# A hybrid decoder block: the last block of the down stages read straight from its accumulator, and the recurrence's gate matmuls on two row halves

## The chip, the core and the metric

The kernel runs on one core of one Trainium2 chip. Its engines work side by side and wait for each other by semaphores: PE (TensorE, matrix products; PEld is its weight load), DVE (VectorE, elementwise work), ACT (ScalarE, activation functions and copies), POOL (GpSimd) and SP (SyncE, which here issues DMAs). Products go to PSUM, an accumulator memory of eight banks; everything else lies in SBUF. The metric is the device time of one execution in microseconds (us); smaller is better.

## What is computed

A block of one layer on 512 tokens of width 1024, all in float32. It is a sum of three steps onto the residual stream, each with a norm before and a norm after:

```python
f = swiglu(rms_norm(h, ffn1_pre_g), ffn1_w_gu, ffn1_w_down)      # width 2816
h = h + 0.5 * rms_norm(f, ffn1_post_g)
m = hybrid_mixer(rms_norm(h, mix_pre_g), ...)
h = h + rms_norm(m, mix_post_g)
f = swiglu(rms_norm(h, ffn2_pre_g), ffn2_w_gu, ffn2_w_down)
h = h + 0.5 * rms_norm(f, ffn2_post_g)
```

The mixer runs a recurrence and a sliding-window attention on the same input and merges them by gates. The recurrence's part that matters here:

```python
xc = causal_depthwise_conv(x_br, conv_w, conv_b)
r = sigmoid(block_diag_linear(xc, w_a, b_a))      # 16 heads of 64 channels, a 64 x 64 matrix each
i = sigmoid(block_diag_linear(xc, w_x, b_x))
log_a = -8 * r * softplus(-lam); a = exp(log_a)
h_t = a_t * h_(t-1) + sqrt(max(1 - a_t**2, 0)) * (i_t * xc_t)
```

## The kernel before, in words

**Products.** Every float32 operand is split into a high part and a low part (a cast on ACT, a subtraction on DVE), and a product is three matmuls: high x high, high x low, low x high (`mm3`, L147 to L150). Weights come from HBM by DMAs on SP (`wload`, L98, three ahead of the splits), are split by `wsplit` (cast L109, subtraction L110), and `wget` (L115) hands them out in one fixed order with two splits ahead.

**The down stages.** The second product of each feed-forward block is done by `down` (L529) as a 2 x 2 block product with seven products instead of eight. Its accumulators are X, Y and Q, each of two banks (two tiles of 128 tokens); products go in the order 1, 2, 3, 6, 5, 7, 4 (L622 to L660). `snap` (L601) copies an accumulator to SBUF, `plus` (L606) adds one to such a copy. Product 7 gives the last of the blocks for tiles 0 and 1, product 4 that for tiles 2 and 3. After product 7, ACT copies X (L645), DVE subtracts the copy "p" and then Q (L647, L648). The whole stretch stands in a block with an order written out by hand (L621): each engine's instructions keep the order in which they are written.

**Closing a stage.** `boundary` (L469) closes each of the three steps; b1 follows the first down stage, b2 the mixer's output product, b3 the second down stage. `half(t, i, z)` (L482) takes half the columns of tile t: a sum of squares on ACT (L489) and the product with the norm's gain on DVE (L490). `epilogue(t)` (L498) computes the inverse norm (a tensor_scalar on DVE, L495, and a power on POOL, L193), adds to the residual (L507), squares again (L512), computes the second inverse norm and multiplies by it and the next gain (L520). Then it hands back a number, FEATURE_LAG, of ticks to wait; a tick is one call of `tick` (L137), made after each piece of weights. Then `to_features` (L202) transposes the tile on PE (L207), casts it to the high part on ACT (L211) and subtracts for the low part on DVE (L212); for b2 it also copies the raw values on ACT (L214). `run` (L123) traces all steps of an epilogue up to that number at once, so they stand in the queues ahead of all that is written later.

In b1 tile 0 waits 6 ticks and tile 1 waits 10. Product 4 takes six pieces for tile 2, then six for tile 3. So tile 0's transposes come right after tile 2's product, and tile 1's after four pieces of tile 3's.

**The mixer.** The first four chunks of the recurrence's input are made by `first_four` (L225), in two halves of the tokens: the first half needs tiles 0 and 1 of the normalised input u2, high and low parts. `lru_chunk` (L817) does a chunk of 128 channels (two heads): convolution (L820 to L823), split (L825, L826), gate matmuls (L836, L837), tanh of each gate (L839, L841), and the factors of the recurrence (L842 to L846). The gate weights are one 128 x 128 matrix per chunk and gate, with the two heads' 64 x 64 matrices on its diagonal and zeros elsewhere. They come by two DMAs of 512 KB (L813), are split at the first chunk (L828 to L831), and each gate of a chunk is one `mm3` into a bank of its own: r in one bank, i in the other, 128 rows each. The last chunk of each group of four starts the scans (L849 to L856).

**Order.** Outside the hand-ordered blocks a planner lists the instructions by its own estimate of times; it may also put instructions from outside into the gaps of a hand-ordered block. PSUM banks and SBUF buffers are given out as they come free.

Of the kernel before, what the change touches and what calls it, by code (L numbers as in the profile page):

```python
# [10 lines left out]
AF = mybir.ActivationFunctionType  # L11
ALU = mybir.AluOpType
# [4 lines left out]
P = 128  # L17
# [2 lines left out]
TAILS = 7  # L20
WARM = 10
JSTD = {"f1": 6, "f2": 4}
FEATURE_LAG = {"b1": (6, 10, 7, 3), "b2": (3, 3, 3, 4)}
ATT_GATES = (2, 3, 4, 5, 6, 7)
T = 512
NT = T // P
D = 1024
# [15 lines left out]
def hybrid_block_kernel(ctx, tc, x, xt, g1, w_first, gains, gu1, gs1, dn1, w_x, w_gate, w_q, w_k, w_v, w_gl, w_ga, w_pl, w_pa,  # L43
# [156 lines left out]
        return u[part][k // 4][:, k % 4, tok]  # L200

    def to_features(un, t, u, name, raw=None):  # L202
        for half in range(2):
            b = bank(f"{name}tp{t}{half}")
            for i in range(4):
                k = 4 * half + i
                PE.transpose(out=b[:, i * P:(i + 1) * P], in_=un[:, k * P:(k + 1) * P], identity=ident)  # L207
# [3 lines left out]
            A.copy(uh, bv)  # L211
            V.tensor_tensor(out=ul, in0=bv, in1=uh.bitcast(F32), op=ALU.subtract)  # L212
            if raw is not None:
                A.copy(raw[half][:, :, ts_], bv)  # L214

    def feat_chunk(b, w, u, tok):
        wh, wl = w
# [251 lines left out]
    def boundary(src, dst, g_post, g_pre, u, scale, name, raw=None, then=None):  # L469
# [7 lines left out]
                rhs.append(rh)  # L477

        cols = (slice(0, 512), slice(512, 1024))
        sq, parts = {}, {}  # L480

        def half(t, i, z, sign=1.0, o=None):  # L482
            if t not in sq:
                sq[t], parts[t] = sm(f"{name}ps{t}", 2), [None, None]
            if o is None:
                while len(rhs) <= t:
                    residual()
                o = rhs[t][:, 1, cols[i]]
            A.activation(t4(f"{name}sq{t}{i}")[:, :512], z, AF.Square, scale=1.0 / 32.0, accum_out=sq[t][:, i:i + 1])  # L489
            V.scalar_tensor_tensor(out=o, in0=z, scalar=sign * scale, in1=g_post[:, cols[i]], op0=ALU.mult, op1=ALU.mult)  # L490
            parts[t][i] = o

        def inverse(ms, z):
            me = sm(f"{name}{z}e")
            V.tensor_scalar(out=me, in0=ms[:, 0:1], scalar1=ms[:, 1:2], scalar2=EPS, op0=ALU.add, op1=ALU.add)  # L495
            return rstd(me, f"{name}{z}r")

        def epilogue(t):  # L498
            while len(rhs) < min(t + 2, NT):
                residual()  # L500
            res, h = rhs[t][:, 0, :], rhs[t][:, 1, :]
            r = inverse(sq[t], f"p{t}")
            yield
            if g_pre is not None:
                ms, un = sm(f"{name}ms{t}", 2), t4(f"{name}un{t}")
            for i in range(2):
                V.scalar_tensor_tensor(out=h[:, cols[i]], in0=parts[t][i], scalar=r, in1=res[:, cols[i]],  # L507
                                       op0=ALU.mult, op1=ALU.add)
                if g_pre is None:
                    (SP if i == 0 else A).dma_start(dst[t][:, cols[i]], h[:, cols[i]])  # L510
                else:
                    A.activation(un[:, cols[i]], h[:, cols[i]], AF.Square, scale=1.0 / 32.0, accum_out=ms[:, i:i + 1])  # L512
            if g_pre is None:
                return
            A.dma_start(dst[t], h)
            yield
            r = inverse(ms, f"n{t}")
            yield
            for i in range(2):
                V.scalar_tensor_tensor(out=un[:, cols[i]], in0=h[:, cols[i]], scalar=r, in1=g_pre[:, cols[i]],  # L520
                                       op0=ALU.mult, op1=ALU.mult)
# [7 lines left out]
    def down(ps, name):  # L529
# [91 lines left out]
        with tc.manual_schedule():  # L621
            for i in (1, 2, 3, 6, 5, 7):  # L622
                for c in range(2 * (i == 1), KS if i < 7 else KS - 3, 2):
                    if i == 7 and c < 4:
                        half(2 + c // 2, 0, sn["a"][c // 2], 1.0, sn["a"][c // 2])
                    if i == 7 and c >= 4:
                        half(c // 2 - 2, 0, sn["c"][c // 2 - 2])
                    piece(i, c)
                if i == 1:
                    snap("a", X)  # L630
                elif i == 2:
                    plus("a", Y)
                elif i == 3:
                    snap("p", Q)
                elif i == 6:
                    snap("c", X)
                elif i == 5:
                    plus("c", Q)
            w = [wget(), wget()]
            prep[7][4]()  # L640
            for t in range(2):
                for c in range(KS - 3, KS):
                    unit(7, c, w[c // (KS - 1)], (t,))
            wsplit(wpos[0] + 4)
            snap("z", X)  # L645
            for t in range(2):
                V.tensor_tensor(out=sn["z"][t], in0=sn["z"][t], in1=sn["p"][t], op=ALU.subtract)  # L647
                V.scalar_tensor_tensor(out=sn["z"][t], in0=Q[t], scalar=-1.0, in1=sn["z"][t], op0=ALU.mult,  # L648
                                       op1=ALU.subtract)
                half(t, 1, sn["z"][t])  # L650
            wsplit(wpos[0] + (KS + 1) // 2)
            run(epilogue(t) for t in range(2))
            ws = []
            for t in range(2):
# [155 lines left out]

    bdt = []
    bdraw = []
    for i in range(2):  # L813
        bdraw.append(t4(f"bdraw{i}"))
        SP.dma_start(bdraw[i], bd[i])

    def lru_chunk(c, b, a4, m4, bx4, last):  # L817
        i = c % 4
# [13 lines left out]
                bdt.append(t)  # L832
        yield LRU_LAG[c // 4]
        cb = slice(c * P, (c + 1) * P)
        br, bi = bank(f"r{c}"), bank(f"i{c}")
        mm3(br, bdt[0][:, 0, cb], bdt[0][:, 1, cb], xh, xl, True, True)  # L836
        mm3(bi, bdt[1][:, 0, cb], bdt[1][:, 1, cb], xh, xl, True, True)  # L837
        tr = t2(f"tr{c}")
        A.activation(tr, br, AF.Tanh, scale=0.5, bias=hb[:, 0, c:c + 1])  # L839
# [263 lines left out]
    dn_run[0].send(boundary(hs2, ov, g_post, None, None, 0.5, "b3"))  # L1103


_VECS = ["conv_b", "lru_b_a", "lru_b_x", "lru_lambda"]


def _layout(inputs):
# [51 lines left out]
    vec = [f["conv_w"][i] for i in range(4)] + [f[n] for n in _VECS]  # L1161
    a["vecs"] = c(np.stack(vec).reshape(8, KD, P).transpose(2, 0, 1))
    bd = np.zeros((2, 2, HD, KD, 2, HD), np.float32)
    wb = np.stack([f["lru_w_a"], f["lru_w_x"]]).reshape(2, KD, 2, HD, HD)
    for r in range(2):
        bd[:, r, :, :, r, :] = wb[:, :, r].transpose(0, 2, 1, 3)
    a["bd"] = bd.reshape(2, P, D)
# [32 lines left out]
```

## Time and profile before

| | us |
|---|---|
| three runs | 1124.97, 1128.05, 1125.46; median 1125.46 |
| the profiled execution | 1124.96 |
| its span, first to last instruction | 1123.2 |
| mean granted TensorE clock in it | 0.997 of full speed |
| PE busy | 1103.9 |
| DVE busy | 896.4 |
| ACT busy | 593.9 |

All times in the rows are counted from the span's start. A row of a timeline has: start, duration, engine, line, operation, output<-inputs, shape, how many rows were merged, and in brackets how long the engine was idle before it and what ended that. A row of the waits has: who waited, for whom, us in total, times, the longest. A row of the windows has: the stretch and its length, then busy time and number of instructions for PE, PEld, DVE, ACT and POOL, then the granted clock, the DMA share and GB/s. A row of a tile has durations in ns (least, median, most), the first and the last start. Matmuls are pipelined: the duration of one is longer than the distance from one start to the next.

### The profile page before, as it was taken

To read this page: it belongs to the slowest core of one execution; us is meant where nothing else is said; L and a number is where in the kernel's file an instruction comes from. 1 tells how busy PE (TensorE), PEld (TensorE's weight loads), DVE (VectorE), ACT (ScalarE), POOL (GpSimd) and SP (SyncE) were. 2 spreads that over 40 slices of the span, in tenths; PEclk is the share of its full clock that TensorE was granted. 3 is DMA by queue.
4 is the path that set the end of the run, shared out by engine and by line. 5 is a ranking of instruction groups with operands and counts; after the bars stand their busy time and mean duration, and the time that the engine had idled before them with its cause. 6 is when DMAs were issued, how large, how long until landed. Compare 5 with 4: busy or idle time off the path is not lost.

```text
span 1123.2 us, 16795 instructions
## 1 busy us (share of the span) xinstructions
PE 1103.9 (98%) x6558; PEld 983.4 (88%) x6558; DVE 896.4 (80%) x1277; ACT 593.9 (53%) x995; POOL 79.5 (7%) x82
## 2 busy tenths in 40 slices
PE   9999999999989999999999999999999999999997
PEld 7889999988868888887888888887999999998885
DVE  6998898888998698999777561556858889888896
ACT  7445555475755658466455341335434455456571
POOL 1000000000001001114022000000000000000000
PEclk9999999999999999999999999999999999999999
DMA  9239999665676272711822340533348999455573
GB/s 359 83 121 261 312 284 302 180 225 150 208 270 213 89 205 76 206 57 57 249 87 86 123 157 31 189 111 113 113 125 261 271 312 282 138 163 189 161 264 113
DMA packets 53279, 202.07 MB, mean 180 GB/s; under 512 B 6352, under 2 KB 6480, under 8 KB 48464
## 3 DMA queue, kind: packets, MB, share of 16 engines
q1 hardware_dynamic: 45424, 163.77, 43.4%
q0 software_dynamic: 3456, 23.07, 10.5%
q10 hardware_dynamic: 4320, 14.16, 3.6%
q8 instruction: 51, 0.84, 0.3%
q14 instruction: 28, 0.23, 0.1%
HBM read 189.44 MB, written 57.67 MB: 220 GB/s over the span
## 4 chain that ended last, share of the span: by engine, by line
PE 84%; DVE 10%; issue 2%; ACT 2%; POOL 1%; DMA 0%; DVEq 0%; POOLq 0%; ACTq 0%
PE f2X L150 4%; PE f2X L149 4%; PE f2X L148 4%; PE f1X L150 4%; PE f1X L149 4%; PE f1X L148 4%; DVE w L110 3%; PE f2Q L150 2%; PE f2Q L149 2%; PE f2Q L148 2%; PE f1Q L150 2%; PE f1Q L149 2%; PE f1Q L148 2%; PE f1f L761 2%; PE x L149 1%
## 5 line engine op out<-in xcount | busy, mean ns | idle before, releaser
L110 DVE TENSOR_TENSOR w<-wraw,w 128x1024 fp32r<-128x1024 f32 x168 | 197.1, 1194 | 38.7 <-ACT w L109 36.9
L109 ACT CAST w<-wraw 128x1024 fp32r<-128x1024 f32 x168 | 163.5, 1011 | 27.7 <-PE glp L150 7.1
L150 PE MATMUL f1X<-u1m,f1W 128*128 128x256 f32 x256 | 72.5, 283 | 0.1
L149 PE MATMUL f1X<-u1m,f1W 128*128 128x256 f32 x256 | 72.4, 283 | 0.0
L148 PE MATMUL f1X<-u1m,f1W 128*128 128x256 f32 x256 | 72.4, 283 | 0.0
L150 PEld LDWEIGHTS f1X<-u1m,f1W 128*128 128x128 f32 x256 | 49.1, 192 | 0.3 <-DVE f1W L316 0.3
L148 PEld LDWEIGHTS f1X<-u1m,f1W 128*128 128x128 f32 x256 | 49.1, 192 | 0.1
L149 PEld LDWEIGHTS f1X<-u1m,f1W 128*128 128x128 f32 x256 | 49.1, 192 | 0.1
L150 PE MATMUL f2X<-u3m,f2W 128*128 128x256 f32 x144 | 40.9, 284 | 0.1
L150 PE MATMUL f2X<-u3h,f2W 128*128 128x256 f32 x144 | 40.8, 283 | 0.0
L148 PE MATMUL f2Q<-u3m,f2W 128*128 128x256 f32 x144 | 40.8, 283 | 0.0
L149 PE MATMUL f2Q<-u3m,f2W 128*128 128x256 f32 x144 | 40.8, 283 | 0.0
L150 PE MATMUL f2Q<-u3m,f2W 128*128 128x256 f32 x144 | 40.8, 283 | 0.0
L149 PE MATMUL f2X<-u3l,f2W 128*128 128x256 f32 x144 | 40.8, 283 | 0.0
L148 PE MATMUL f2X<-u3m,f2W 128*128 128x256 f32 x144 | 40.8, 283 | 0.0
L149 PE MATMUL f2X<-u3m,f2W 128*128 128x256 f32 x144 | 40.7, 283 | 0.0
L148 PE MATMUL f2X<-u3h,f2W 128*128 128x256 f32 x144 | 40.7, 283 | 0.0
L148 PE MATMUL f1Q<-u1m,f1W 128*128 128x256 f32 x128 | 36.2, 283 | 0.0
L149 PE MATMUL f1Q<-u1m,f1W 128*128 128x256 f32 x128 | 36.2, 283 | 0.0
L150 PE MATMUL f1Q<-u1m,f1W 128*128 128x256 f32 x128 | 36.2, 283 | 0.0
L149 PE MATMUL f1X<-w,f1y 128*128 128x512 f32 x88 | 35.0, 397 | 0.6 <-DVE w L110 0.6
L148 PE MATMUL f1X<-w,f1y 128*128 128x512 f32 x88 | 35.1, 398 | 0.0
(847 smaller groups left out, 3753.9 us busy)
## 6 DMA issues: line engine op xcount, KB each, us to landing
wraw<-wsum SPq DMA_DIRECT2D x40, 512.0 KB, 4.0
wsum<-in_dn_dram SPq DMA_DIRECT2D x16, 1024.0 KB, 9.0
wraw<-in_dn_dram SPq DMA_DIRECT2D x30, 512.0 KB, 5.0
f2L<-in_gs_dram SPq DMA_DIRECT2D x18, 512.0 KB, 5.0
f2R<-in_gs_dram SPq DMA_DIRECT2D x18, 512.0 KB, 5.1
wraw<-in_gu_dram SPq DMA_DIRECT2D x16, 512.0 KB, 5.8
f1L<-in_gs_dram SPq DMA_DIRECT2D x16, 512.0 KB, 5.5
f1R<-in_gs_dram SPq DMA_DIRECT2D x16, 512.0 KB, 5.7
```

The source lines that it names most:

```text
L109: A.copy(w[:, 0, :], raws[n])
L110: V.tensor_tensor(out=w[:, 1, :], in0=raws[n], in1=w[:, 0, :].bitcast(F32), op=ALU.subtract)
L148: PE.matmul(o, lhsT=ah, rhs=bh, start=start, stop=False, skip_group_check=reopen)
L149: PE.matmul(o, lhsT=ah, rhs=bl, start=False, stop=False, skip_group_check=reopen)
L150: PE.matmul(o, lhsT=al, rhs=bh, start=False, stop=stop, skip_group_check=reopen)
L761: PE.matmul(bs[i], lhsT=lw[:, i * P:(i + 1) * P], rhs=rx, start=k == 0 and n == 0, stop=k == KD - 1 and n == 2)
```

## The change

- **Down stages.** Q - p is computed right after product 5, into p. After product 7 one operation per tile takes -X - p straight from the accumulator; the copy of X and one subtraction per tile are gone. All six weight splits of product 4 are asked for ahead of the last matmuls of product 7 instead of four ahead and two behind the halves. The first halves of tiles 2 and 3 are done at product 6, those of tiles 0 and 1 at the first two pieces of product 7.
- **`half` and `epilogue`.** For the second half of the columns the gain is kept back and done in the epilogue, behind the tensor_scalar and the issue of the power. This holds at all three closings.
- **`to_features`.** Where raw copies are wanted, they come after both halves' casts and subtractions.
- **FEATURE_LAG.** b1: tile 0 waits 7 ticks and tile 1 waits 9; b2: tile 3 waits 3.
- **The gates.** The weights are one 128 x 1024 array: the rows are a head's 64 input channels for the even heads, then for the odd ones; for each chunk the columns are 64 outputs of gate r and 64 of gate i. A chunk's matmuls use 64 rows each, alternately of the first and the second head, and each head has its own bank with r in the lower half of the partitions and i in the upper half. The two tanh over 128 partitions become four over 64, two of which write to another half than they read. One DMA, one cast and one subtraction load the weights instead of two each. The biases are laid out to match.

```diff
-FEATURE_LAG = {"b1": (6, 10, 7, 3), "b2": (3, 3, 3, 4)}
+FEATURE_LAG = {"b1": (7, 9, 7, 3), "b2": (3, 3, 3, 3)}
...
     def to_features(un, t, u, name, raw=None):
+        keep = []
...
             if raw is not None:
-                A.copy(raw[half][:, :, ts_], bv)
+                keep.append((raw[half][:, :, ts_], bv))
+        for z, bv in keep:
+            A.copy(z, bv)
...
-        sq, parts = {}, {}
+        sq, parts, late = {}, {}, {}
...
             A.activation(t4(f"{name}sq{t}{i}")[:, :512], z, AF.Square, scale=1.0 / 32.0, accum_out=sq[t][:, i:i + 1])
-            V.scalar_tensor_tensor(out=o, in0=z, scalar=sign * scale, in1=g_post[:, cols[i]], op0=ALU.mult, op1=ALU.mult)
             parts[t][i] = o
+
+            def gain():
+                V.scalar_tensor_tensor(out=o, in0=z, scalar=sign * scale, in1=g_post[:, cols[i]], op0=ALU.mult,
+                                       op1=ALU.mult)
+
+            if i == 0:
+                gain()
+            else:
+                late[t] = gain
...
             r = inverse(sq[t], f"p{t}")
+            late[t]()
             yield
...
                 for c in range(2 * (i == 1), KS if i < 7 else KS - 3, 2):
+                    if i == 6 and c < 4:
+                        half(2 + c // 2, 0, sn["a"][c // 2], 1.0, sn["a"][c // 2])
                     if i == 7 and c < 4:
-                        half(2 + c // 2, 0, sn["a"][c // 2], 1.0, sn["a"][c // 2])
-                    if i == 7 and c >= 4:
-                        half(c // 2 - 2, 0, sn["c"][c // 2 - 2])
+                        half(c // 2, 0, sn["c"][c // 2])
                     piece(i, c)
...
                 elif i == 5:
                     plus("c", Q)
+                    for t in range(2):
+                        V.tensor_tensor(out=sn["p"][t], in0=Q[t], in1=sn["p"][t], op=ALU.subtract)
             w = [wget(), wget()]
             prep[7][4]()
+            wsplit(wpos[0] + (KS + 1) // 2)
             for t in range(2):
                 for c in range(KS - 3, KS):
                     unit(7, c, w[c // (KS - 1)], (t,))
-            wsplit(wpos[0] + 4)
-            snap("z", X)
             for t in range(2):
-                V.tensor_tensor(out=sn["z"][t], in0=sn["z"][t], in1=sn["p"][t], op=ALU.subtract)
-                V.scalar_tensor_tensor(out=sn["z"][t], in0=Q[t], scalar=-1.0, in1=sn["z"][t], op0=ALU.mult,
-                                       op1=ALU.subtract)
-                half(t, 1, sn["z"][t])
-            wsplit(wpos[0] + (KS + 1) // 2)
+                z = sn["p"][t]
+                V.scalar_tensor_tensor(out=z, in0=X[t], scalar=-1.0, in1=z, op0=ALU.mult, op1=ALU.subtract)
+                half(t, 1, z)
             run(epilogue(t) for t in range(2))
...
-    for i in range(2):
-        bdraw.append(t4(f"bdraw{i}"))
-        SP.dma_start(bdraw[i], bd[i])
+    bdraw.append(t4("bdraw"))
+    SP.dma_start(bdraw[0], bd)
...
-        br, bi = bank(f"r{c}"), bank(f"i{c}")
-        mm3(br, bdt[0][:, 0, cb], bdt[0][:, 1, cb], xh, xl, True, True)
-        mm3(bi, bdt[1][:, 0, cb], bdt[1][:, 1, cb], xh, xl, True, True)
+        heads = (slice(0, HD), slice(HD, P))
+        bs = [bank(f"ri{c}{r}") for r in range(2)]
+        for n, (w, x) in enumerate(((0, xh), (0, xl), (1, xh))):
+            for r, own in enumerate(heads):
+                PE.matmul(bs[r], lhsT=bdt[0][own, w, cb], rhs=x[own, :], start=n == 0, stop=n == 2)
         tr = t2(f"tr{c}")
-        A.activation(tr, br, AF.Tanh, scale=0.5, bias=hb[:, 0, c:c + 1])
         ti = bx4[:, i, :]
-        A.activation(ti, bi, AF.Tanh, scale=0.5, bias=hb[:, 1, c:c + 1])
+        for z, o in enumerate((tr, ti)):
+            for r, own in enumerate(heads):
+                A.activation(o[own, :], bs[r][heads[z], :], AF.Tanh, scale=0.5, bias=hb[heads[z], r, c:c + 1])
```

The rest of the diff lays out the gate weights and the biases in that order on the host.

More of the change, by code (lines that the diff above doesn't have):

```diff
@@ L1103, in hybrid_block_kernel @@
     dn_run[0].send(boundary(hs2, ov, g_post, None, None, 0.5, "b3"))
-_VECS = ["conv_b", "lru_b_a", "lru_b_x", "lru_lambda"]
 def _layout(inputs):
@@ L1160, in _layout @@
     a["dn2"] = down_blocks(f["ffn2_w_down"])
-    vec = [f["conv_w"][i] for i in range(4)] + [f[n] for n in _VECS]
+    gates = np.stack([f["lru_b_a"], f["lru_b_x"]]).reshape(2, KD, 2, HD).transpose(2, 1, 0, 3).reshape(2, D)
+    vec = [f["conv_w"][i] for i in range(4)] + [f["conv_b"], gates[0], gates[1], f["lru_lambda"]]
     a["vecs"] = c(np.stack(vec).reshape(8, KD, P).transpose(2, 0, 1))
-    bd = np.zeros((2, 2, HD, KD, 2, HD), np.float32)
     wb = np.stack([f["lru_w_a"], f["lru_w_x"]]).reshape(2, KD, 2, HD, HD)
-    for r in range(2):
-        bd[:, r, :, :, r, :] = wb[:, :, r].transpose(0, 2, 1, 3)
-    a["bd"] = bd.reshape(2, P, D)
+    a["bd"] = c(wb.transpose(2, 3, 1, 0, 4).reshape(P, D))
     a["sinks"] = f["attn_sinks"]
```

## The prediction

> **What bounds the kernel now.** I read the page first, then the waits of PE, then the timeline of each stage where PE waits, because only there can a change of order pay.
>
> ```profile
> span 1123.2 us, 16795 instructions
> ...
> PE 1103.9 (98%) x6558; PEld 983.4 (88%) x6558; DVE 896.4 (80%) x1277; ACT 593.9 (53%) x995; POOL 79.5 (7%) x82
> ```
>
> TensorE is busy in 98% of the span. So there are two ways to gain: take matmul time away, or take away one of the few waits of PE. The waits of PE, longest first (us in total, times, longest):
>
> ```profile
> PE b1ntp L207 <- DVE b1un L520: 4.8, 2, 3.8
> PE f2f L148 <- ACT u3h L211: 1.5, 1, 1.5
> ...
> PE q L148 <- DVE at01pl L978: 1.3, 1, 1.3
> PE at02t L975 <- POOL at02s L969: 1.2, 1, 1.2
> PE f1X L149 <- DVE w L110: 0.6, 1, 0.6
> PE f2X L149 <- DVE w L110: 0.6, 1, 0.6
> PE f2f L149 <- DVE u3l L212: 0.4, 1, 0.4
> ```
>
> The first row, the join of the first feed-forward block to the mixer (b1), is the largest. The two rows of w L110 are the start of the last product of the two down stages. The rows of f2f are the join b2. The rows of q and at02t stand in the mixer, where DVE has a backlog. PE at b1:
>
> ```profile
> 332.24 0.39 PE L150 MATMUL f1X<-w,f1y 128*128 128x512 f32 x1
> 336.39 1.32 PE L207 MATMUL b1ntp<-ident,b1un 128*128 128x128 f32 x8 [3.76 <-DVE b1un L520]
> ...
> 338.10 0.63 PE L150 MATMUL f1X<-w,f1y 128*128 128x512 f32 x1
> ...
> 340.66 0.63 PE L150 MATMUL f1X<-w,f1y 128*128 128x512 f32 x1
> ...
> 347.33 0.39 PE L150 MATMUL f1X<-w,f1y 128*128 128x512 f32 x1
> ...
> 350.82 0.29 PE L149 MATMUL x<-u2l,w 128*128 128x256 f32 x1
> ```
>
> PE stands at tile 0's transposes for 3.8 us. After that seven matmuls, from 338.10 to 340.66, start 0.43 us apart instead of 0.227 (1.36 us for six, shown below): the granted clock was halved after the pause, and that costs 7 x 0.2 = 1.4 us more. Then the mixer's first product does not run freely until 350.82.
>
> **The down stages.** What DVE and ACT do before those transposes:
>
> ```profile
> 321.70 2.35 DVE L110 TENSOR_TENSOR w<-wraw,w 128x1024 fp32r<-128x1024 f32 x2
> ...
> 324.69 0.69 DVE L648 SCALAR_TENSOR_TENSOR f1z<-f1Q,f1z 128x512 f32<-128x512 f32 x1
> ...
> 329.23 1.83 DVE L110 TENSOR_TENSOR w<-wraw,w 128x1024 fp32r<-128x1024 f32 x2 [1.07 <-ACT w L109]
> 330.98 0.20 DVE L495 TENSOR_SCALAR b1p0e<-b1ps 128x1 f32<-128x1 f32 x1
> ...
> 331.93 1.42 DVE L507 SCALAR_TENSOR_TENSOR b1rh<-b1rh,b1p0r 128x512 f32<-128x512 f32 x2 [0.62 <-POOL b1p0r L193]
> ...
> 335.60 1.40 DVE L520 SCALAR_TENSOR_TENSOR b1un<-b1rh,b1n0r,g_b 128x512 f32<-128x512 f32 x2
> ...
> 338.24 2.35 DVE L110 TENSOR_TENSOR w<-wraw,w 128x1024 fp32r<-128x1024 f32 x2
> ...
> 342.43 2.35 DVE L110 TENSOR_TENSOR w<-wraw,w 128x1024 fp32r<-128x1024 f32 x2
> 345.22 0.75 DVE L507 SCALAR_TENSOR_TENSOR b1rh<-f1a,b1p2r,b1rh 128x512 f32<-128x512 f32 x1 [0.44 <-POOL b1p2r L193]
> ...
> 348.56 1.41 DVE L520 SCALAR_TENSOR_TENSOR b1un<-b1rh,b1n2r,g_b 128x512 f32<-128x512 f32 x2 [0.66 <-POOL b1n2r L193]
> 349.89 1.28 DVE L212 TENSOR_TENSOR u2l<-b1ntp,u2h 128x512 fp32r<-128x512 f32 x2
> ```
> ```profile
> 324.22 0.59 ACT L604 COPY f1z<-f1X 128x512 f32<-128x512 f32 x1 [1.45 <-PE f1X L150]
> 325.48 0.63 ACT L489 ACTIVATE b1sq<-f1z 128x512 f32<-128x512 f32 x1 [0.67 <-DVE f1z L648]
> 326.01 0.19 ACT L489 ACTIVATION_READ_ACCUMULATOR b1sq<-f1z 128x1 f32 x1
> ```
>
> ACT copies the second part of X at 324.22, as soon as PE has finished it; DVE is at its splits until 321.70 + 2.35 = 324.05, so the two arrive together. The change removes, behind the last matmul of product 7, two copies on ACT and two subtractions on DVE (the latter move ahead of product 7). The two gains of the second halves move behind the tensor_scalar, beside POOL's power. The two splits of 329.23 come forward. The working for the changed order:
>
> DVE ends its four splits at 324.05 + 1.83 = 325.9; X is complete by then, so it does L648 twice and is free at 327.3. ACT squares tile 0 from 326.6 and tile 1 from 327.4, each 0.63 and 0.19 for reading the sum, and ends at 328.2. DVE then does tensor_scalar, gain, tensor_scalar, gain and reaches L507 at about 329.0, against 331.93. That is 2.9 us earlier. The same pattern follows, so L520 has its first half ready at 336.3 - 2.9 = 333.4 (336.3 is 335.60 and half of 1.40). PE's last matmul of tile 0 gives way at 332.24 + 0.23 = 332.5; without the 0.6 us wait for L110 that is 331.9, and the lag of 7 gives it one more piece of six matmuls: 333.2. The wait at the transposes falls from 3.8 to 0.2 us, much shorter than the pause behind which the clock was halved. PE reaches the end of tile 1 at 347.6 - 0.6 - 3.6 - 1.4 = 342.0.
>
> What is late next is tile 2's chain. With the lag of 7 the casts L211 and L212 of tiles 0 and 1 stand on ACT and DVE behind all of tile 2's epilogue, and the mixer's first product waits for the low parts of both tiles. DVE ends L520 of tile 1 at 338.3 - 2.9 = 335.4 (the next splits start at 338.24), two splits at 337.7, then tensor_scalar and gain at 338.5. Before, L507 of tile 2 stood until 345.22, because POOL's power stood beside the two splits of 342.43. Without them it begins at 338.6, L520 follows 3.3 us later as in the trace (345.22 to 348.56) at 341.9 and ends at 343.2. The third of four L212 at 0.6 each ends at 345.0. The first product then runs from 345.2 instead of 350.82: 5.6 us gained. Those splits are not in the hand order, though; a planner puts them into gaps. If these two and a third fall in again, at 1.17 each less the little gap that they fill, they take about 3.1 us and leave 2.5. I take **4.5**, nearer the first, since the gain now fills one of these gaps. The bounds are 2.5 and 5.8 (all of 0.6, 3.8 and 1.4).
>
> In the second down stage the L110 wait of **0.6** goes: all six splits are done before product 4, on DVE time that the two subtractions and two copies leave. At its end:
>
> ```profile
> 1117.07 0.69 DVE L490 SCALAR_TENSOR_TENSOR b3rh<-f2X,g_b 128x512 f32<-128x512 f32 x1 [2.11 <-ACT b3sq L489]
> ...
> 1118.61 0.75 DVE L507 SCALAR_TENSOR_TENSOR b3rh<-f2a,b3p3r,b3rh 128x512 f32<-128x512 f32 x1 [0.73 <-POOL b3p3r L193]
> ```
>
> The gain L490 stands in front of the tensor_scalar; behind it, it lies beside POOL's power. L507 starts **0.6** earlier, and the last store with it. If POOL were held by the gain, nothing would be gained there.
>
> At b2 the copies L214 go behind both casts and tile 3's lag is one tick less. Between losing both f2f waits (1.9 gained) and holding a bank for two reads longer (2 x 0.63 = 1.3 lost) I take **0.5** gained, since the planner, not the trace, sets this order.
>
> **The gates.**
>
> ```profile
> 439.00 0.39 PE L148 MATMUL r<-xch,bd 128*128 128x512 f32 x1
> ...
> 440.36 0.39 PE L148 MATMUL q<-u2h,w 128*128 128x512 f32 x1
> ```
> ```profile
> L148 PE MATMUL r<-xch,bd x8: 389/389/396, 374.0 to 439.0; 128*128 128x512 f32 x8
> ...
> L839 ACT ACTIVATE tr<-r,hb x8: 672/685/690, 376.5 to 439.9; 128x512 f32<-128x512 f32 x8
> ```
> ```profile
> 416.00:443.00 27.00, 27.00 (x121) 22.36 (x120) 20.09 (x27) 21.02 (x31) 1.65 (x2) 1.00 0.34 114
> 443.00:463.00 20.00, 20.00 (x93) 16.61 (x91) 19.84 (x23) 10.54 (x12) 4.79 (x3) 1.00 0.51 141
> ```
> ```profile
> 461.73 1.21 DVE L110 TENSOR_TENSOR w<-wraw,w 128x1024 fp32r<-128x1024 f32 x1
> ...
> 463.31 0.45 PE L150 MATMUL gt<-u2h,w 128*128 128x512 f32 x1
> ```
>
> Six matmuls of a chunk take 1.36 us, 0.227 each; eight chunks take 10.9. Afterwards there are as many matmuls, but each uses 64 rows, and two neighbours use different rows and different banks. No row of this trace shows a matmul with 64 rows. If the pair runs side by side, 24 x 0.227 = 5.4 us of PE go. If one follows the other, nothing goes. If besides PE runs empty at each change of form, 0.389 - 0.227 = 0.16 us is lost 16 times, 2.6 in all. I take the pairing: neither of the two needs what the other holds.
>
> The Trainium skill (TensorEngine Tiling (Array Packing), Key Properties) speaks against the full gain: changing the tiling mode drains the array. By it PE would gain 5.4 - 2.6 = 2.8 us, the sum below would be 9.0 and the time 1116.0. Nothing in this trace shows such a drain.
>
> ACT pays for it: two more tanh per chunk, 0.685 each, 5.5 us for a group of four chunks. In the second group's stretch (416 to 443) ACT is busy 21.0 of 27.0. Afterwards it has 26.5, in a stretch that PE shortens to 24.3, and is 2.2 us over. So chunk 7's gates are out 5.4 - 2.2 = 3.2 us earlier, not 5.4. From there DVE has no slack: it is busy 19.84 of 20 us, and the split it ends at 462.94 is read at 463.31. PE that comes earlier waits for it, and the waits of q and at02t (2.5 us) stay. Net: **3.2**. The bounds are 5.4 (ACT fits its idle time) and, without pairing, a loss of 1.4, as chunk 7's two extra tanh (2 x 0.685) delay DVE's backlog; with drains, 2.6.
>
> One load of the gate weights instead of two takes one cast and one subtraction of 128x1024 (1.2 us on DVE) and one DMA on SP away. PE waits for none of them: nothing, and at most 1.2 gained.
>
> Sum: 4.5 + 0.6 + 0.6 + 0.5 + 3.2 = 9.4 us. The profiled execution took 1124.96 (its span of 1123.2 and 1.8 around it), which gives 1115.6. The median of the runs is 0.5 higher, within their spread of 3.1.
>
> **The rivals.**
> (1) The row halves don't run side by side. For it: no such matmul in the trace. The gates then lose 1.4, and the sum is 6.2 - 1.4 = 4.8: 1120.2; with drains (2.6 lost) 1121.4.
> (2) The b1 gain is taken back at the mixer's first product: the planner's splits fall into tile 2's chain again, and the pause halves the clock as it did at 338. For it: the three splits stand there now. b1 brings 2.5 - 1.4 = 1.1, the sum is 6.0: 1119.0.
> (3) Everything fits: b1 5.8, the gates 5.4, the rest 1.7: 12.9, so 1112.1; with both f2f waits gone (1.4 more) 1110.7. For it: DVE's idle time before 443, in which the planner may place work; against it: the 0.37 us at 463.
> (4) ACT becomes the bound of the recurrence. Its idle time there is waiting for PE and cannot be filled, so each extra tanh lies on the path: 16 x 0.685 = 11.0 us more in place of 3.2 less, and 1124.96 - 6.2 + 11.0 = 1129.8, slower than before. It decides once the chunk's chain on ACT is longer than the PE time between two chunks. Against it: ACT has 6 us idle in the second group's stretch.
> (5) The change does not do what it says: the planner, which sets the order outside the hand-ordered stages, fills the time again with waits elsewhere: about 1125. For it: DVE is busy in 80% of the span and seldom far behind PE.
>
> **How the numbers follow.** Forecast 0.48 (1115.6), rival 1 0.14, rival 2 0.19, rival 3 0.09, rival 4 0.05, rival 5 0.05. The range goes from rival 3 (1110) to rival 1 with drains (1121.5); it leaves out rivals 4 and 5 and a little of the edges. Under about 0.3%, 3.4 us, a measurement cannot tell this kernel from no change. Forecast, rival 2, rival 3 and nearly all of rival 1 are beyond that: faster 0.85. Rival 5 and a rest of rival 1 are the same: 0.09. Rival 4 and a part of 5: slower 0.06.
>
> **What would show it.** In the changed profile the L110 waits of f1X and f2X are gone from PE's list, the b1ntp row falls below 1.5 us, the matmuls after the transposes keep 0.227, and the mixer's first low-part matmul starts near 345. The two matmuls of a gate pair start within 0.05 us of each other. PE waits longer in the mixer behind DVE (gt, q or at02t) by about 2 us. The forecast is wrong if the pairs start 0.227 apart, if the first x product still starts after 349, or if ACT stands on the chain through the recurrence.

## The result and the profile after

The changed kernel takes 1131.82 us (median; 1130.52 to 1133.24), the kernel before beside it 1125.11 (1124.43 to 1128.05). The ratio is 1.006, with a 95% interval of 1.005 to 1.007: slower by 6.7 us, where 9.4 us less were forecast. Three of its six runs took 1130.5 to 1130.7, with a granted clock of 0.998 or 0.999 of full speed, and three 1132.9 to 1133.2, with 0.993 or 0.994. The profiled execution took 1130.52. The tail of product 7 is L661 now (before L648), the gain L496 (L490), the closing's operations L506, L519 and L532 (L495, L507, L520), the gate matmuls L849 and their tanh L854.

The page's span and engines, and the waits of PE (us in total, times, longest):

```profile
span 1128.7 us, 16793 instructions
...
PE 1106.0 (98%) x6558; PEld 977.5 (87%) x6558; DVE 894.1 (79%) x1276; ACT 602.7 (53%) x1006; POOL 79.2 (7%) x82
```
```profile
PE gt L150 <- DVE w L110: 3.3, 3, 1.6
PE at02t L988 <- POOL at02s L982: 2.5, 1, 2.5
PE f1X L148 <- DVE f1p L661: 2.3, 1, 2.3
PE f2X L148 <- DVE f2p L661: 2.3, 1, 2.3
...
PE f2f L148 <- ACT u3h L212: 1.2, 1, 1.2
...
PE f2f L149 <- DVE u3l L213: 0.5, 1, 0.5
```

The row of b1ntp, 4.8 us before, is gone, and so are the two L110 rows of the down stages. Two new rows of 2.3 us stand for f1X and f2X. In the mixer gt (a product) and at02t (transposes of the attention) wait longer. PE's busy time has grown by 2.1 us although a pair of gate matmuls now runs together.

PE at product 4 of the first down stage, and DVE beside it:

```profile
323.94 0.39 PE L150 MATMUL f1X<-w,f1y 128*128 128x512 f32 x1
326.68 0.47 PE L148 MATMUL f1X<-w,f1y 128*128 128x512 f32 x1 [2.34 <-DVE f1p L661]
...
328.23 0.63 PE L148 MATMUL f1X<-w,f1y 128*128 128x512 f32 x1
...
330.79 0.63 PE L148 MATMUL f1X<-w,f1y 128*128 128x512 f32 x1
...
346.39 0.28 PE L149 MATMUL x<-u2l,w 128*128 128x256 f32 x1
```
```profile
321.84 4.09 DVE L110 TENSOR_TENSOR w<-wraw,w 128x1024 fp32r<-128x1024 f32 x4
325.85 1.28 DVE L661 SCALAR_TENSOR_TENSOR f1p<-f1X,f1p 128x512 f32<-128x512 f32 x2
...
328.83 1.41 DVE L519 SCALAR_TENSOR_TENSOR b1rh<-b1rh,b1p0r 128x512 f32<-128x512 f32 x2
...
332.50 1.41 DVE L532 SCALAR_TENSOR_TENSOR b1un<-b1rh,b1n0r,g_b 128x512 f32<-128x512 f32 x2
...
341.44 1.42 DVE L532 SCALAR_TENSOR_TENSOR b1un<-b1rh,b1n2r,g_b 128x512 f32<-128x512 f32 x2 [0.66 <-POOL b1n2r L193]
```

Product 4 accumulates into X, and its first matmul may not write there until L661 has read it. DVE comes to L661 only behind four splits, so PE stands from 324.2 to 326.7. Seven matmuls from 328.23 to 330.79 then start 0.43 us apart: the clock is halved again, now behind this pause. The granted clock of that stretch is 0.50 (third number from the end):

```profile
328.00:331.40 3.40, 3.40 (x10) 2.63 (x9) 3.40 (x7) 1.73 (x5) 1.32 (x2) 0.50 0.81 305
```

The recurrence: PE around the first gate matmuls of the changed kernel, then ACT over one chunk, first of the kernel before, then of the changed one, where the last row is the first tanh of the last chunk.

```profile
369.40 0.28 PE L150 MATMUL x<-u2h,w 128*128 128x256 f32 x1
369.62 0.50 PE L849 MATMUL ri<-xcl,bd 64*128 64x512 f32 x2
369.95 0.40 PE L849 MATMUL ri<-xch,bd 64*128 64x512 f32 x2
370.28 0.39 PE L148 MATMUL x<-u2h,w 128*128 128x256 f32 x1
...
371.55 0.49 PE L849 MATMUL ri<-xch,bd 64*128 64x512 f32 x2
...
378.54 0.50 PE L849 MATMUL ri<-xch,bd 64*128 64x512 f32 x2
```
```profile
375.95 0.69 ACT L841 ACTIVATE lb<-i,hb 128x512 f32<-128x512 f32 x1 [2.08 <-PE i L150]
376.54 0.68 ACT L839 ACTIVATE tr<-r,hb 128x512 f32<-128x512 f32 x1
377.11 0.78 ACT L820 ACTIVATE xc<-x,vec 128x512 f32<-128x512 f32 x1
...
382.27 0.68 ACT L841 ACTIVATE lb<-i,hb 128x512 f32<-128x512 f32 x1
```
```profile
370.38 1.39 ACT L854 ACTIVATE tr<-ri,hb 64x512 f32<-64x512 f32 x2 [1.01 <-PE ri L849]
371.80 1.39 ACT L854 ACTIVATE lb<-ri,hb 64x512 f32<-64x512 f32 x2
373.21 0.78 ACT L830 ACTIVATE xc<-x,vec 128x512 f32<-128x512 f32 x1
...
378.37 1.39 ACT L854 ACTIVATE tr<-ri,hb 64x512 f32<-64x512 f32 x2
...
442.59 0.68 ACT L854 ACTIVATE tr<-ri,hb 64x512 f32<-64x512 f32 x1 [0.48 <-PE ri L849]
```

A row of a pair (x2) spans 0.49 us, so the two matmuls lie beside each other. But the run of two pairs takes 0.76 us from the matmul before (369.40 and its 0.12) to the one behind: 0.29 more than two pairs at 0.236 each. ACT needs 2.83 us for the four tanh (370.38 to 373.21) where two took 1.16 (375.95 to 377.11). From the first tanh of the first chunk to the first of the second it works without a gap, 7.99 us where it was 6.32. The next such distance is 6.81 (6.63 before). PE starts on the second and the third chunk 7.0 us apart (371.55 and 378.54). One chunk does not settle which engine is behind, so here are the two groups of four chunks, each from its first tanh to the end of its last, before and after:

```profile
375.95:393.28 17.33, 17.33 (x88) 14.69 (x87) 13.63 (x20) 15.23 (x23) 0.45 (x1) 1.00 0.20 61
421.28:441.13 19.85, 19.85 (x89) 16.42 (x89) 14.60 (x21) 16.37 (x24) 0.00 (x0) 1.00 0.24 81
```
```profile
370.38:393.01 22.63, 22.63 (x127) 17.54 (x128) 15.20 (x20) 21.66 (x31) 2.37 (x2) 1.00 0.14 47
421.02:445.38 24.36, 24.21 (x107) 17.48 (x107) 15.71 (x22) 22.81 (x32) 0.61 (x1) 1.00 0.19 65
```

ACT has 6.4 us more to do in each group, 12.9 in all. Its idle time falls from 2.1 and 3.5 us to 1.0 and 1.5 and so takes up 3.1 of them; the other 9.8 make the groups longer. The first chunk's first tanh comes 5.6 us earlier than before (370.38 against 375.95), the last chunk's 2.7 later (442.59 against 439.88).

Who then waits: DVE for the gates' tanh, between 365 and 450, before and after, and the engines by stretch (PE, PEld, DVE, ACT, POOL busy) after.

```profile
DVE lb L842 <- ACT lb L841: 6.3, 3, 2.1
```
```profile
DVE lb L855 <- ACT lb L854: 10.7, 6, 3.1
```
```profile
416.00:443.00 27.00, 26.84 (x117) 19.03 (x118) 16.95 (x23) 23.05 (x32) 0.00 (x0) 1.00 0.28 102
443.00:463.00 20.00, 18.22 (x78) 14.05 (x77) 20.00 (x25) 14.59 (x18) 6.92 (x4) 1.00 0.49 143
```

DVE does 16.95 us of work in the stretch to 443, where it did 20.09 before. In the next 20 us it is busy throughout and cannot catch up, and PE, which was never idle there before, waits for it (18.22 of 20).

### The profile page after: what moved, and what is told of

Its sections match the earlier page's. It is cut to its first block, busy times and chain, and to the rows that moved or that the text cites. A ratio compares the mean times of both kernels' runs of the same rounds, so it can differ in the third digit from the quotient of the medians.

```text
span 1128.7 us, 16793 instructions
## 1 busy us (share of the span) xinstructions
PE 1106.0 (98%) x6558; PEld 977.5 (87%) x6558; DVE 894.1 (79%) x1276; ACT 602.7 (53%) x1006; POOL 79.2 (7%) x82
## 4 chain that ended last, share of the span: by engine, by line
PE 84%; DVE 9%; ACT 3%; issue 2%; DMA 1%; POOL 0%; DVEq 0%; POOLq 0%; ACTq 0%; SPq 0%
PE f2X L150 4%; PE f2X L148 4%; PE f2X L149 4%; PE f1X L150 4%; PE f1X L148 4%; PE f1X L149 4%; DVE w L110 3%; PE f2Q L150 2%; PE f2Q L149 2%; PE f2Q L148 2%; PE f1Q L150 2%; PE f1Q L148 2%; PE f1Q L149 2%; PE f1f L772 2%; PE glg L148 1%
## 5 line engine op out<-in xcount | busy, mean ns | idle before, releaser
L110 DVE TENSOR_TENSOR w<-wraw,w 128x1024 fp32r<-128x1024 f32 x168 | 197.2, 1197 | 31.1 <-ACT w L109 29.9
L148 PE MATMUL f1X<-w,f1y 128*128 128x512 f32 x88 | 35.3, 401 | 2.3 <-DVE f1p L661 2.3
L148 PE MATMUL f2X<-w,f2y 128*128 128x512 f32 x88 | 34.3, 390 | 2.3 <-DVE f2p L661 2.3
```

The costliest lines, as they stand in the source:

```text
L110: V.tensor_tensor(out=w[:, 1, :], in0=raws[n], in1=w[:, 0, :].bitcast(F32), op=ALU.subtract)
L148: PE.matmul(o, lhsT=ah, rhs=bh, start=start, stop=False, skip_group_check=reopen)
```

## The experiments

The theory after the first comparison: **A**, the loss is made in the recurrence, because ACT sets its pace, and the stages gain although they pay for the wait at product 4. The rivals: **B**, the direct read of the accumulator is what makes the kernel slower; **C**, any new order that the planner makes costs.

**e1, e2: the two halves of the change apart.** e1 is the changed kernel with the gate lines of the kernel before, e2 the kernel before with the gate lines of the changed one.

> The down stages, the closings and the lags as changed, the gates as before. Theory A (the loss is made in the recurrence by the gates; the stages pay one wait, for X to be read, and still gain): about 1121.5, that is 3 to 4 us under before, since the changed kernel stood 4.25 us ahead at its first product of k, and lost 1.6 and won 0.5 in the second down stage. Theory B (the direct read of X is what makes it slower, the lead at k is an accident of one profile): 1127 to 1131. Theory C (any new order of the planner costs some us in the mixer): 1125 to 1129, with waits of PE behind DVE at gt as in the changed kernel.

> The gates as changed, all else as before. Theory A: 1132 to 1134, the 8 us that PE fell back between the first product of k and the fifth of gt. Theory B: 1122 to 1125. Theory C: 1125 to 1129.

e1 took 1121.59 us, ratio 0.9975 (0.9965 to 0.9986); e2 1135.58, ratio 1.0085 (1.0071 to 1.0099); the kernel before 1124.99. So -3.4 and +10.6, which make 7.2 where 6.7 were measured. The loss is the gates', and theory B falls as far as the whole goes: the stages gain. PE's 2.3 us at f1X and f2X stand in e1 as well. Not all of the 10.6 is waiting: the trace of e2 has two stretches of 3.4 us at half clock in the mixer (from 457.7 and 529.3) that neither the kernel before nor the traced run of the changed kernel has. From the mixer's first key product (kk) to its first product into the tile glg, behind the recurrence, the traces of the kernel before, the changed kernel and e2 take 159.9, 168.8 and 170.7 us.

**e3, e4: the two halves of the gates apart.** e3 is the kernel before with each tanh issued as two of 64 partitions, e4 has the row halves and two tanh of 128, so r and i of the two heads are exchanged in part and the recurrence computes something else.

```diff
-        A.activation(tr, br, AF.Tanh, scale=0.5, bias=hb[:, 0, c:c + 1])
         ti = bx4[:, i, :]
-        A.activation(ti, bi, AF.Tanh, scale=0.5, bias=hb[:, 1, c:c + 1])
+        for z, (o, b2) in enumerate(((tr, br), (ti, bi))):
+            for own in (slice(0, HD), slice(HD, P)):
+                A.activation(o[own, :], b2[own, :], AF.Tanh, scale=0.5, bias=hb[own, z, c:c + 1])
```

> The kernel before with each tanh of the gates done as two of 64 partitions, nothing else: ACT's part of the change alone. If ACT's two extra tanh per chunk are the cost (theory A): 1130 to 1133. If the form of the matmuls is the cost, through what it loses at each change of form: 1124.5 to 1126.

> The kernel before with the gate matmuls on row halves and two tanh of 128 partitions, one per bank; the r and i of the two heads are then exchanged in part, so the recurrence computes something else with the same instructions. PE's part alone. Theory A: 1124 to 1126, since the 48 matmuls took 10.6 us in the changed kernel and 10.9 before. If the form of the matmuls is the cost: 1130 or more. If the drains went away with the other order, as much as 5 us under before.

e3 took 1136.01, ratio 1.0096 (1.0082 to 1.0109): +11.0, with every matmul as before. ACT's extra tanh alone make a loss as large as the whole gate change. In the stretch from kk to glg e3 takes 168.9 us, 9.0 more than the kernel before; outside it, its trace has two more stretches at half clock (from 349.4 and 793.2), about 1.5 us each. e4 took 1128.43, ratio 1.0025 (1.0017 to 1.0034): +3.4. Its gate matmuls took 9.9 us in 15 runs, against 10.9 before, so PE saves 1.0 us of work, and the kernel is slower all the same. Three of its eleven runs, with the clock at 0.997, lost only 1.4 to 1.9 us; the traced one, at 0.995, has a stretch at half clock behind a wait at q (from 515.4). The two halves do not add up: 11.0 and 3.4 against the 10.6 of e2.

**e7, e11: is e4's loss one of form or of order?** e7 issues the gate matmuls of the kernel before, 128 rows each, as r, i, r, i, r, i; e11 issues i, i, i, r, r, r.

> The kernel before with its gate matmuls, 128 rows each as before, issued r, i, r, i, r, i instead of r, r, r, i, i, i; nothing else. So both banks are full together and the first tanh can start only after five of the six matmuls instead of three. Theory A (row halves cost by themselves: the run with row halves and two tanh of 128 partitions, 1128.43, lost its 3.4 us to changes of the matmul's form): 1125 within 0.7. Rival C (what it lost is the later first tanh and the planner's new order): 1127 to 1129.

> The kernel before with the i gate's three matmuls issued ahead of the r gate's three; the same instructions, nothing else, a control for the run with r and i interleaved (1128.8). Theory C1 (any new order that the planner makes of the recurrence costs 2 to 4 us, the order before being a lucky one): 1127 to 1129. Theory C2 (the interleaving cost because both gates are complete only after all six): r is complete later still, so 1127 or more as well if the r gate's chain is the long one, but 1125 within 0.7 if what counts is the first tanh of either gate.

e7 took 1128.80 (1127.28 to 1131.07), ratio 1.0035 (1.0022 to 1.0048); e11 1125.26, ratio 1.0003 (0.9994 to 1.0012). C in its wide form falls: another order by itself costs nothing. But the interleaving costs as much as e4 did, without a row half, so e4's loss cannot be put down to the 64-row form. Not all of e7's loss is the gates', either: in its trace, of a run of 1130.59, about 1.5 us are lost at half clock behind the transposes, from 349.7 to 353.1, before the first gate matmul. As much is lost from 523.8 to 527.2, behind a wait for POOL at at02t, and the waits of q and at02t are 2.0 us longer than before (4.5 against 2.5). Why the interleaving makes these waits longer stays open.

**e6: the direct read alone.** The kernel before, with product 3 minus product 5 taken ahead, and

```diff
-            snap("z", X)
             for t in range(2):
-                V.tensor_tensor(out=sn["z"][t], in0=sn["z"][t], in1=sn["p"][t], op=ALU.subtract)
-                V.scalar_tensor_tensor(out=sn["z"][t], in0=Q[t], scalar=-1.0, in1=sn["z"][t], op0=ALU.mult,
-                                       op1=ALU.subtract)
-                half(t, 1, sn["z"][t])
+                z = sn["p"][t]
+                V.scalar_tensor_tensor(out=z, in0=X[t], scalar=-1.0, in1=z, op0=ALU.mult, op1=ALU.subtract)
+                half(t, 1, z)
```

> The kernel before with one part of the change: the last block is formed straight from the accumulator, product 3 minus product 5 is taken ahead, and ScalarE's copy goes; the order of the splits, the early squares, the gains, the lags, the casts and the gates stay as before, so two splits stand ahead of the read. Theory A (the direct read is cheap, and what costs is the place of the splits): TensorE waits 0.3 to 0.8 us for the read in each down stage and the join wins back some VectorE time: 1122 to 1124.5. Rival B (reading the accumulator that the next product writes is itself what costs): a wait of 1.5 us or more in each down stage, 1126 or more.

It took 1127.66, ratio 1.0026 (1.0016 to 1.0036): as rival B said. Its PE waits, and the copy of the kernel before:

```profile
PE f1X L148 <- DVE f1p L649: 1.8, 1, 1.8
PE f2X L148 <- DVE f2p L649: 1.8, 1, 1.8
```
```profile
322.18 0.59 ACT L604 COPY f1z<-f1X 128x512 f32<-128x512 f32 x1 [2.32 <-PE f1X L150]
```

ACT had stood idle for 2.32 us and gave X back at 322.8, ahead of product 4. The copy looked like work to save, but it was what let PE go on. The direct read hands that duty to DVE, which has splits in front of it. Part of the 2.9 us is the clock: e6's trace has two stretches at half clock that the kernel before lacks, one from 349.3 and one from 1103.7, behind the wait at f2X.

**e5, e8: the read earlier, a first try.** e5 is e1 with one split ahead of the first read instead of four, and each tile's read and square placed right behind its last matmul. e8 is the changed kernel with the same edit.

> The stages of the change with the old gates (1121.59 us in its own run), with one edit: in the last quarter of product 7, VectorE reads each tile's accumulator as soon as that tile's matmuls are in, with one weight split ahead of the first read instead of four, and the other three splits after it. Theory A (TensorE's 2.3 us at product 4 is the wait for that read, made by the splits queued ahead of it, and the half clock behind it follows from the pause): the waits for the accumulator go in both down stages (2 x 2.3), the 1.4 us at half clock go, some 0.5 to 1.5 us come back at the transposes of tiles 0 and 2, which are then early: 1116 to 1118.5. Rival B (VectorE has the same work before the join, so the wait only moves to the splits or to the transposes): 1120.5 to 1122.

> The changed kernel with the one edit of e5 (VectorE reads each tile's accumulator behind one split instead of four); gates as changed. Theory A (the stages' waits and the gates' loss add up): it gains what e5 gains on the stages alone, 3 to 5 us, so 1127 to 1129, still slower than before, by the gates. Rival C (the recurrence's backlog starts earlier when the stages end earlier, and eats it): 1130.5 to 1132.

e5 took 1123.80, ratio 0.9992 (0.9983 to 1.0001), e8 1133.11, ratio 1.0071 (1.0058 to 1.0084): both 1.3 to 2.2 us worse than without the edit. The wait at product 4 was gone, but the transposes waited 4.1 us. ACT and DVE of e5 show why:

```profile
323.71 0.63 ACT L492 ACTIVATE b1sq<-f1p 128x512 f32<-128x512 f32 x1 [4.05 <-DVE f1p L660]
...
324.34 1.03 ACT L109 CAST w<-wraw 128x1024 fp32r<-128x1024 f32 x1
```
```profile
325.41 1.23 DVE L110 TENSOR_TENSOR w<-wraw,w 128x1024 fp32r<-128x1024 f32 x1 [1.79 <-ACT w L109]
```

The edit had put ACT's square, which waits for DVE, in front of ACT's cast, for which DVE's next split waits. Each engine held the other.

**e9, e10: the read earlier, in the right order.** e9 is e5 with both squares behind all casts. e10 keeps ACT's copies, one ahead of the last two casts and one behind, and forms the block from the copy.

```diff
             prep[7][4]()
-            wsplit(wpos[0] + (KS + 1) // 2)
+            wsplit(wpos[0] + 3)
             for t in range(2):
                 for c in range(KS - 3, KS):
                     unit(7, c, w[c // (KS - 1)], (t,))
-            for t in range(2):
                 z = sn["p"][t]
                 V.scalar_tensor_tensor(out=z, in0=X[t], scalar=-1.0, in1=z, op0=ALU.mult, op1=ALU.subtract)
-                half(t, 1, z)
+                wsplit(wpos[0] + 4 + 2 * t)
+            for t in range(2):
+                half(t, 1, sn["p"][t])
```

> As e5 (stages alone, VectorE's first read of the accumulator behind one split), but ScalarE's squares of the last block are issued behind its casts of the weights instead of between them. In e5 the casts stood behind the squares, each square waited for VectorE, and VectorE's splits then waited 1.79 us twice for the casts: the closings began at 330.8 us instead of 326.3. Theory A (that queue was the whole loss of e5): the splits end near 326 us, TensorE's waits for the accumulator and the half clock stay away, the transposes of tile 0 wait about 0.5 us and of tile 2 about 1 us: 1116 to 1119. Rival B (the closings on VectorE bound the join whatever TensorE does in product 4): 1120.5 to 1122.

> The stages of the change with the old gates, but the accumulator is copied by ScalarE as in the kernel before, one copy ahead of the last two casts and one behind them, and VectorE forms the last block from the copy with one subtraction instead of two; order of the splits, squares, gains and lags as changed. So product 4 waits for ScalarE, which is idle there, not for VectorE. Theory A (what the direct read costs is that a busy engine holds the accumulator; the gain of the stages is the shorter closing): no wait above 0.5 us at product 4 in either down stage, 1116 to 1119. Rival B (the direct read itself is what gains): 1121.5 or more.

e9 took 1116.41, ratio 0.9928 (0.9915 to 0.9940), e10 1116.94, ratio 0.9932 (0.9919 to 0.9944): both beat both kernels, by some 8 us the one before. DVE and PE's waits in e9:

```profile
322.04 0.68 DVE L660 SCALAR_TENSOR_TENSOR f1p<-f1X,f1p 128x512 f32<-128x512 f32 x1
322.64 1.22 DVE L110 TENSOR_TENSOR w<-wraw,w 128x1024 fp32r<-128x1024 f32 x1
323.77 0.68 DVE L660 SCALAR_TENSOR_TENSOR f1p<-f1X,f1p 128x512 f32<-128x512 f32 x1
324.37 1.82 DVE L110 TENSOR_TENSOR w<-wraw,w 128x1024 fp32r<-128x1024 f32 x2
326.11 0.21 DVE L506 TENSOR_SCALAR b1p0e<-b1ps 128x1 f32<-128x1 f32 x1
```
```profile
PE x L148 <- ACT u2h L212: 0.4, 1, 0.4
PE b1ntp L208 <- DVE b1un L532: 0.3, 1, 0.3
```

The first read stands at 322.04, before product 4 begins at 323.24. DVE reaches the closing at 326.1 with the same operations as in the changed kernel, and the waits of f1X and f2X are gone. e10 shows that who reads X does not matter, as long as it comes early: theory B falls for good.

**e12: the lags of the joins put back** in e1.

> The stages of the change with the old gates (1121.59), with the lags of the join put back to 6, 10, 7, 3 and 3, 3, 3, 4. Theory A (the stages gain by VectorE's shorter closings; the lags only follow): within 1 us of 1121.6. Rival D (moving the transposes is what gains): 1123.5 or more, with a wait of the first transposes of over 1 us.

It took 1124.09, ratio 0.9992 (0.9983 to 1.0001), 2.5 us more than e1, as rival D said; but its mechanism does not show. The transposes wait 0.3 us, and at the mixer's first key product e12 stands 3.8 us ahead of the kernel before, e1 3.9. What sets the two traces apart is product 4 of the second down stage: behind the same pause of 2.34 us the clock was halved in e12 for seven matmuls and not in e1. All eleven runs of e12 show a clock of 0.995 or 0.996; of e1's seven, five show 0.998, and the two at 0.996 took 1123.6 and 1123.8, as long as e12. What the lags are worth is not settled.

**e13, e14: the gates on top of the mended stages.** e13 is the changed kernel with the edit of e9, e14 the same with two tanh of 128 partitions.

> The changed kernel with the one mend of e9 (VectorE's first read of the accumulator behind one split, ScalarE's squares behind its casts); gates as changed. Theory A (stages and gates add up: mended stages 1116.4, the gates alone 1135.6 against 1125.0, so 10.6): 1125.5 to 1128, no faster than the kernel before. Rival C (the recurrence's backlog waits for work that the earlier stages feed, so what the stages gain is lost in it): 1130 or more.

> As e13, but with two tanh of 128 partitions a chunk instead of four of 64: the two heads' r and i values are partly exchanged, so the recurrence computes something else in the same time; it leaves out the change's extra ScalarE work and keeps its 64-row matmuls. Theory A (ScalarE's tanh make the loss; the row halves by themselves cost what they cost in the kernel before, 3.4): 1118.5 to 1121. Rival E (that 3.4 belonged to the old join, and with an early join the saved TensorE time of about 1 us shows): 1115 to 1116.5.

e13 took 1126.67, ratio 1.0016 (1.0007 to 1.0025), e14 1119.13, ratio 0.9945 (0.9932 to 0.9959); the kernel before took 1125.31 beside them. Against e9 the gates cost 10.3 us, of which the row halves carry 2.7 and the two more tanh 7.5. Both are theory A's numbers: the gates' loss stands on its own. It needs no change of the clock either: the traces of e9 and e13 show none at half clock between the first down stage and the tail, and from kk to glg they take 159.4 and 168.9 us (e14 161.9).

## Why the prediction was wrong

**The gates: the step that failed.** The prediction took 3.2 us gained; e2 measured 10.6 lost, 13.8 of the 16.1 us by which the forecast missed. Two things were wrong in it.

The term for ACT compared two more tanh per chunk with ACT's idle time in the second group's stretch, 21.0 of 27.0 us. It left out the first group's:

```profile
376.00:403.00 27.00, 27.00 (x166) 24.26 (x165) 23.35 (x30) 24.66 (x36) 3.01 (x2) 1.00 0.24 79
```

There the kernel before has 2.3 us to spare for 5.5. And a share of a stretch was the wrong measure: the conv, the cast, the gate matmuls, the tanh and the exponential of a chunk follow each other, and ACT carries most of that chain. So its idle time took up only 3.1 of the 12.9 us of added work. The gates of chunk 7, the last, were forecast 3.2 us earlier; their first tanh came 2.7 later. DVE's scans come later with them, and PE waits for DVE after 443. This is rival 4, which had a chance of 0.05: ACT becomes the bound of the recurrence. Its condition (ACT's pass longer than PE's) shows in the first pass (7.99 against 7.0) and not in the second (6.81). That its price, 16 x 0.685 = 11.0, is what e3 measured (11.0) is in part luck: the sixteen tanh made 12.9 us of ACT's work in the changed kernel, not all of it lay on the path, and some 3 us of e3's trace are half clock outside the recurrence.

The term for PE, 5.4 gained, was sized as if runs cost nothing. The pairs do run side by side, 0.24 us for both. But every run of them costs 0.29 us besides, and the planner cuts three pairs of a chunk into about two runs (15 in all): 10.6 us in the changed kernel, 0.7 of it waiting, against 10.9. So PE gained 0.3. The prediction had bounded such a loss at 0.16 for each change of form, 2.6 in all, and left it out of the sum. Two changes at 0.16 are near the 0.29 of a run; that there would be fifteen runs, not eight, it did not see. A cost for each run speaks for the rule of the Trainium skill that the prediction weighed (TensorEngine Tiling (Array Packing), Key Properties: a change of the tiling mode drains the array): the trace agrees, with 0.29 us for entering and leaving together, though it shows the time lost and not what the array does in it.

**The first down stage: the total nearly right, by another way.** 4.5 was forecast; at the mixer's first key product (372.0 against 376.2) the changed kernel was 4.25 ahead. DVE's working held: L519 at 328.83 (forecast 329.0), L532 at 332.50 (its first half was forecast ready at 333.4), tile 2's at 341.44 (341.9), the first x product with low parts at 346.39 (345.2). But the working put L648 behind four splits, at 325.9, and asked only who needs its result, not who waits for what it reads. Tile 0's transposes were forecast at 333.2, as if product 4 could start at once, and came at 337.25: PE lost 2.3 us there, and 1.4 at half clock. The shorter closing paid for both, and that the total came out near is luck: in e9, where neither is left, the lead at the same place is 6.6. Rival 2 had a halved clock, but at the transposes.

**The second down stage: wrong in sign.** The L110 wait went, as forecast (0.6), but the same four splits in front of L661 made product 4 begin 2.5 us later. From its first product to its last matmul the stage went from 4.5 us behind the kernel before to 6.1: 1.6 lost where the prediction gained 0.6.

**The tail and b2: right.** The gain beside POOL's power:

```profile
1123.18 0.21 DVE L506 TENSOR_SCALAR b3p3e<-b3ps 128x1 f32<-128x1 f32 x1 [5.12 <-ACT b3sq L492]
...
1124.12 0.75 DVE L519 SCALAR_TENSOR_TENSOR b3rh<-f2a,b3p3r,b3rh 128x512 f32<-128x512 f32 x1
```

From the first of the closing's operations to L519 it takes 0.94 us (1.54 before): 0.6 gained, as forecast. At b2 the f2f waits fell from 1.9 to 1.7: 0.2 instead of 0.5.

**What was said to show it.** The b1ntp row and the L110 rows fell away and the pairs start together, as forecast; PE waits longer for DVE and POOL in the mixer, as forecast but for another cause. Of the three signs of a wrong forecast the last one came, ACT on the chain through the recurrence. The chain of waits of the changed kernel from 365 to 450, by line; in the kernel before the same answer begins with PE's x, v and kk and has no ACT among its first twelve:

```profile
by line: ACT lb L854 6.5%; ACT tr L854 6.4%; ACT w L109 5.6%; DVE lm L868 5.4%; PE ri L849 5.3%; DVE xc L832 5.2%; PE kk L148 4.8%; PE kk L149 4.5%; PE kk L150 4.0%; DVE w L110 4.0%; ACT la L856 3.9%; ACT tr L857 3.8%; issue 3.4%; DVE lb L8
```

## What to carry to other kernels

When a step that reads an accumulator is moved or handed to another engine, ask which matmul waits for the read to be over, and where the reader's queue stands at that moment: a copy on an idle engine can be cheaper than no copy on a busy one. And where work of equal chunks passes from engine to engine, compare the engines' time from chunk to chunk, not their busy share of a stretch: here an engine with a fifth of a stretch to spare took up a quarter of the added work, and the rest made the chain longer.

## What the runs showed of the hardware

- A tanh on 64 partitions lasts as long as one on 128 (0.683 and 0.685 us). In a row they cost more: four follow each other at 0.71 us, where the two of 128 stood 0.58 apart.
- Two 64-row matmuls on the two row halves run together, a further pair every 0.24 us, but a run of them between 128-row matmuls costs 0.29 us besides: 0.52 for one pair, 0.75 for two, about 1.0 for three.
- Behind pauses of PE the granted clock fell to 0.50 for 3.4 us at a time (328.0 to 331.4 in the changed kernel), but not each time. The pause at product 4, 2.34 us, was followed by seven matmuls at half clock in some places and not in others (in the changed kernel and in e1 in the first down stage alone, in e12 in both). Behind the waits at gt (0.28, 0.22 and 1.3 us within 3.3) and at at02t (2.5) it fell in e2 and e8, and not in the traced run of the changed kernel, which has the same waits. The Trainium skill (TensorE: Matmul & The Clock Gate, What's actually happening) has the clock fall after at least one idle window of about 3.4 us; here a pause of 2.34 us was enough, at times, and so were the three short ones at gt.
